# A two-layer fp32 decoder trunk: new opening and last unit, sums by adding DMAs, two more seven-product pairs and new orders

## The chip, the cores and the metric

The kernel runs on one core of a Trainium2 chip. Times are microseconds on the device, of whole executions; the profile shows one execution. In the text TensorE is PE in the rows, VectorE is DVE, ScalarE is ACT, GpSimd is POOL and SyncE is SP. GpSimd issues the DMAs that convert a type or add into their destination; the other DMAs are issued by SyncE, or ScalarE.

## The reference, cut to what matters

Two layers over 256 rows x of 2048 values, all in float32. Almost all of the work is in the matrix products: w_in (2048 x 6160), w_o (2048 x 2048), w_up (2048 x 8192) and w_down (8192 x 2048) in each layer. Every value is asked for to float32 accuracy.

```python
def hybrid_layer(x, ...):
    h = rms_norm(x, attn_norm)
    proj = jnp.einsum('bsd,de->bse', h, w_in)
    g_q, g_k, g_v, g_gate, g_lr, s_q, s_k, s_v = jnp.split(proj, COL_SPLITS, axis=-1)
    ...
    mixed = jnp.concatenate([o_gla, o_sb], axis=-1)
    x = x + jnp.einsum('bse,ed->bsd', mixed, w_o)
    hm = rms_norm(x, mlp_norm)
    up = jnp.square(jax.nn.relu(jnp.einsum('bsd,df->bsf', hm, w_up)))
    return x + jnp.einsum('bsf,fd->bsd', up, w_down)
```

## The kernel before

**A float32 product is three matmuls.** Operand and weight are each split in a rounded high part and the low part that the rounding left. High by high, high by low weight and low by high weight are summed in a PSUM bank (lines 630 to 632 in the opening, 1231, 1234 and 1235 in the planned part), each a 128x512 matmul. High parts (whi) are made by ScalarE, low parts (wlo) by VectorE with one subtraction. The weights of two pairs in each unit are split by DMA instead: a casting DMA makes chi (line 1059), ScalarE copies it negated into dlo (line 1063), and a DMA that adds the weight to dlo leaves the low part there (line 1066). GpSimd issues both in program order.

**Units, pairs and steps.** A unit is 2048 rows of a weight by 1024 columns: eight pairs of 128-row blocks, into up to eight PSUM banks. A pair takes eight products (24 matmuls, two steps) or, as a "fast" pair, seven (21 matmuls, four steps): products of sums of blocks, in the way of Strassen and Winograd, for which VectorE makes one sum of 128x1024 and two of 128x512 (line 876) and some more low parts. The operand's sums are made once for each of its pairs and kept (table `FAST_OF` by operand: `ht` for h, `sxh` and `sx` for the MLP's). The banks of a fast unit aren't yet results: the unit's tail adds them into four quarters of 128x512, two row halves by two column halves.

**The tables set the order.** A table for each kind of unit (`EACH`, `FEWER`, `LATER`, `O0`, `O1`, `OWN`) holds the order of the steps by pair number, the fast pairs, and the pairs that are split by DMA. `LATER` is for the key and query units `ik` and `iq` that run at the end of layer 0 and belong to layer 1's input product (around 1110 to 1190 us). The class `Plan` (line 63) takes the pieces of all units with their lengths and due times. PE, SP and POOL follow the order in which the program names their pieces; VectorE and ScalarE take, of the pieces that can start, the one that is due first.

**The drain of a down unit.** `seeded_tail` (line 1295) first puts x's own values into banks 2, 4, 3 and 8 (seeds). When the products are done, ScalarE copies bank 1 into x11, VectorE makes the difference dw of bank 6 and x11 in a temporary (one of `T2` = 5), and so on in `sums`; `half` (one for each column half c) adds banks 2 and 3 on VectorE, and copies banks 4 and 8 on ScalarE, after which VectorE adds bank 5 to the latter and dw to both. In the last unit of the kernel each quarter is stored from there (line 1346).

**The opening.** x, the gains (line 337) and the first weights are loaded on SP's queue in this order. `wait_on_x(WARM0)` lets TensorE turn the identity 8 times. `norm_operand` (line 507 for the turns, 517 for the high parts on ScalarE, 523 for the low ones on VectorE) makes the first two blocks of h out of x; between its turns and its high parts `turn_gains` (line 346) turns the gains into columns. `wait_on_x(WARM1)` is 13 more turns of the identity (line 580). Then come the first products.

Of the kernel before, what the change touches and what calls it, by code (L numbers as in the profile page):

```python
# [11 lines left out]
F32R = mybir.dt.float32r  # L12
BF16 = mybir.dt.bfloat16
AF = mybir.ActivationFunctionType
ALU = mybir.AluOpType
# [1 line left out]

P = 128
EPS = 1e-6
WARM0, WARM1 = 8, 13  # L20
T2 = 5
FAST = (1, 3, 5, 6)
EACH = [7, 7, 1, 1, 0, 1, 2, 5, 2, 5, 5, 3, 5, 3, 3, 4, 6, 1, 6, 6, 6, 3, 4, 0], FAST, (2, 4)
FEWER = [0, 0, 2, 1, 1, 1, 4, 1, 7, 7, 6, 6, 2, 6, 6, 3, 3, 3, 5, 3, 4, 5], (1, 3, 6), (2, 4)
LATER = [4, 0, 0, 1, 1, 4, 1, 1, 3, 3, 3, 2, 6, 3, 6, 6, 6, 5, 5, 5, 5, 2, 7, 7], FAST, (2, 4)
FAST_OF = {"ht": FAST, "sxh": (0, 1, 3, 5, 6), "sx": (0, 1, 3, 5, 6)}
TWO_WAYS = (("sxh", 0), ("sx", 0))
O0 = [4, 4, 7, 7, 6, 6, 0, 0, 0, 0, 5, 1, 1, 1, 2, 5, 1, 2, 2, 2, 3, 3], (0, 1, 2), (5, 7)
O1 = [4, 5, 4, 2, 2, 2, 2, 6, 1, 1, 0, 0, 1, 1, 0, 0, 6, 5, 7, 7, 3, 3], (0, 1, 2), (5, 6)
SEEDED = (("down", 0), ("down", 1), ("o", 1))  # L30
SPARE = ("sxh",)
OWN = {
    ("up", 0): ([2, 6, 6, 6, 6, 3, 3, 3, 3, 4, 1, 1, 5, 1, 2, 1, 5, 5, 5, 0, 4, 0, 0, 0, 7, 7], (0, 1, 3, 5, 6), (2, 4)),
    ("up", 0, 0): ([0, 0, 1, 4, 1, 1, 5, 1, 5, 2, 3, 5, 3, 3, 5, 2, 3, 6, 6, 6, 6, 4, 7, 7], FAST, (2, 4)),
    ("up", 1): ([0, 0, 3, 3, 4, 3, 3, 5, 5, 5, 6, 5, 2, 6, 6, 6, 1, 1, 2, 1, 1, 7, 4, 7], FAST, (2, 4)),
    ("down", 0): ([0, 0, 3, 3, 1, 4, 3, 3, 1, 5, 1, 2, 1, 5, 5, 5, 2, 6, 6, 6, 6, 4, 7, 7], FAST, (2, 4)),
    ("down", 1): ([7, 7, 3, 3, 2, 3, 3, 1, 1, 1, 2, 1, 0, 0, 0, 0, 5, 5, 4, 5, 5, 6, 6, 6, 6, 4], (0, 1, 3, 5, 6), (2, 4)),
}
CAST, AHEAD_BY = 3, 1
FIRST_RAWS = 6  # L40
RING, LOWS, ADDS, RAWS = 5, 4, 2, 3
# [21 lines left out]
class Plan:  # L63
# [29 lines left out]
    def run(self):  # L93
# [20 lines left out]
        line = {e: [p for p in self.pieces if p.engine == e] for e in ("PE", "SP", "POOL")}  # L114
# [3 lines left out]
        ready = {"DVE": [], "ACT": []}  # L118
        order, events, count = [], [], 0
        left_tiles, sure = T2, 0  # L120
        for p in self.pieces:
# [53 lines left out]
def trunk_kernel(  # L175
# [90 lines left out]
    def f32(ap):  # L266
        return ap.bitcast(F32)

    nc.scalar.preload_act_table_set("natural_log_exp_and_others")


    ident = cpool.tile([P, P], F32, name="ident")
# [178 lines left out]
    def forms(op, i, t, tag):  # L451

        both = (tag, i) in TWO_WAYS
        keep = tag is None or both

        e = []
        todo = []

        a11, a21, a12, a22 = (t[:, k, r * P : (r + 1) * P] for k in range(2) for r in range(2))

        def new(k):
            if not e:
                n = 4 if keep else 3
                e.append(tmp("t2", [P, 512], bufs=T2)[:, : n * P].rearrange("p (k c) -> p k c", c=P))
            return a21 if k == 3 and not keep else e[0][:, k, :]

        def sums(k):
            a, b = ((a21, a11), (a21, a22), (a11, new(3)), (a12, new(0)))[k]  # L470
            nc.vector.tensor_tensor(new((2, 3, 0, 1)[k]), a, b, ALU.subtract)

        def high():
            if e:
                if both:
                    if tag in SPARE:
                        op.x[i] = act_tile(F32R, (P, 4, 2, P))
                    else:
                        op.x[i] = tmp(tag + "k", [P, 4, 2, P], F32R, bufs=1)
                elif keep:  # L480
                    op.x[i] = act_tile(F32R, (P, 4, 2, P))
                else:
                    op.x[i] = tmp(tag, [P, 3, 2, P], F32R, bufs=4)
# [375 lines left out]
    def ordered(l, units, hT, rst, ug, gates_t, mixed=None, ons=None):  # L859
# [23 lines left out]
        def unit_order(u):  # L883

            kind, q, n2 = units[u]
            if kind == "g":
                return [i // 2 for i in range(8)], (), ()
            if kind == "o":
                return (O0, O1)[n2]
            if u and units[u - 1][0] == "down" and kind == "iv":  # L890
                return FEWER
            if l >= 0 and kind in AHEAD:
                return LATER
            return OWN.get((kind, n2, q), OWN.get((kind, n2), EACH))

        def added(u, j):
# [398 lines left out]
        def seeded_tail(u):  # L1295
            kind, q, n2 = units[u]
            end = kind == "down" and q == 3 and l + 1 == DEPTH
            x11, x21, x12, x22 = (
                (lambda ap=xb[2 * n2 + c][:, tt, :]: ap) for c in range(2) for tt in range(2)
            )  # L1300
# [13 lines left out]
            def sums(p):  # L1314
# [6 lines left out]
                b = vector(dw, bk(7), dw, a, p[7])  # L1321
                free.update({1: [c], 6: [w], 5: [a], 7: [b]})
                box["s"] = (w, b, a, b)

            def half(c, p):
                got = []
                for tt, (m, dst) in enumerate((((2, x11), (4, x21)), ((3, x12), (8, x22)))[c]):
                    before = [p[m], seeds[m]]
# [324 lines left out]
    his = []  # L1653
    load_x(0, parts=2)
    load_gains(0, (("attn", attn_norm, KT),))
    wait_on_x(WARM0)
    st["first"] = norm_operand(hT, 0, "attn", 0, lambda: turn_gains(0))
    wait_on_x(WARM1)
# [316 lines left out]
```

## Time and profile before

| | us |
|---|---|
| median of 3 runs | 2124.44 |
| lowest and highest of them | 2122.53, 2124.86 |
| time of the profiled execution | 2122.05 |
| its span in the trace | 2120.2 |
| TensorE busy in it | 2111.3 |

The span counts from the first to the last event of the trace. The profiled execution's own time is 1.85 us more than its span, which lies around it. TensorE's time counts a 128x512 matmul with 0.39 us, though the next begins earlier: rates are to be read from one start to the next.

### The profile page before, as it was taken

To read this page: it belongs to the slowest core of one execution; us is meant where nothing else is said; L and a number is where in the kernel's file an instruction comes from. 1 tells how busy PE (TensorE), PEld (TensorE's weight loads), DVE (VectorE), ACT (ScalarE), POOL (GpSimd) and SP (SyncE) were. 2 spreads that over 40 slices of the span, in tenths; PEclk is the share of its full clock that TensorE was granted. 3 is DMA by queue.
4 is the path that set the end of the run, shared out by engine and by line. 5 is a ranking of instruction groups with operands and counts; after the bars stand their busy time and mean duration, and the time that the engine had idled before them with its cause. 6 is when DMAs were issued, how large, how long until landed. Compare 5 with 4: busy or idle time off the path is not lost.

```text
span 2120.2 us, 28343 instructions
## 1 busy us (share of the span) xinstructions
PE 2111.3 (100%) x10040; PEld 1758.5 (83%) x10040; DVE 1936.9 (91%) x2658; ACT 1498.6 (71%) x2032; POOL 273.6 (13%) x394
## 2 busy tenths in 40 slices
PE   9999999999999999999999999999999999999998
PEld 7888888888888888888888888888888888888887
DVE  6988769999999999999998886799999999999998
ACT  7667667777677677677776665677776776776775
POOL 1110001111111111111111000111112111111110
PEclk9999999999999999999999999999999999999999
DMA  9865367888888988988998644778889888889886
GB/s 318 257 184 188 111 198 221 231 268 260 250 245 246 263 250 251 258 258 244 253 266 240 189 138 135 211 220 252 259 244 255 261 251 254 245 250 261 249 253 191
DMA packets 157618, 497.15 MB, mean 234 GB/s; under 512 B 10682, under 2 KB 19458, under 8 KB 157476
## 3 DMA queue, kind: packets, MB, share of 16 engines
q1 hardware_dynamic: 100900, 319.16, 42.2%
q0 software_dynamic: 56576, 176.18, 37.0%
q8 instruction: 79, 1.29, 0.2%
q14 instruction: 63, 0.52, 0.1%
HBM read 493.20 MB, written 2.10 MB: 234 GB/s over the span
## 4 chain that ended last, share of the span: by engine, by line
PE 76%; issue 17%; POOL 2%; DVE 1%; DMA 1%; ACT 1%; POOLq 0%; ACTq 0%
PE acc L630 3%; PE acc L632 3%; PE acc L631 3%; POOL dlo L1066 1%; POOL chi L1059 1%; DMA raw<-in_w_up_dram 1%; DMA dlo<-in_w_down_dram 1%; DVE wlo L613 0%; PE ps L741 0%; PE ps L759 0%; PE ps L1912 0%; ACT whi L611 0%; DVE t L1767 0%; PE ps L1862 0%; PE ps L795 0%
## 5 line engine op out<-in xcount | busy, mean ns | idle before, releaser
L1102 DVE TENSOR_TENSOR wlo<-raw,whi 128x1024 fp32r<-128x1024 f32 (+1 forms) x697 | 751.2, 1084 | 67.9 <-ACT whi L1098 45.5
L1098 ACT ACTIVATE whi<-raw 128x1024 fp32r<-128x1024 f32 (+1 forms) x697 | 648.3, 946 | 193.3 <-DVE raw L876 83.0
L1063 ACT ACTIVATE dlo<-chi 128x1024 fp32r<-128x1024 f32 x168 | 177.7, 1058 | 106.5 <-DMA chi<-in_w_down_dram 12.7
L1098 ACT ACTIVATE whi<-ts 128x1024 fp32r<-128x1024 f32 x177 | 187.6, 1060 | 84.2 <-DVE ts L876 69.9
L1102 DVE TENSOR_TENSOR wlo<-ts,whi 128x1024 fp32r<-128x1024 f32 x177 | 215.7, 1219 | 4.7 <-PE m__244_1205 L1234 2.7
L876 DVE TENSOR_TENSOR ts<-raw 128x1024 f32<-128x1024 f32 x177 | 215.8, 1219 | 2.7 <-DMA raw<-in_w_up_dram 1.8
L630 PE MATMUL acc<-whi,act 128*128 128x512 f32 (+2 forms) x384 | 141.3, 368 | 0.0
L632 PE MATMUL acc<-whi,act 128*128 128x512 f32 (+2 forms) x384 | 136.7, 356 | 0.0
L631 PE MATMUL acc<-wlo,act 128*128 128x512 f32 (+2 forms) x384 | 136.4, 355 | 0.0
L611 ACT ACTIVATE whi<-raw 128x1024 fp32r<-128x1024 f32 (+2 forms) x98 | 88.5, 909 | 64.4 <-PE acc L632 63.4
L613 DVE TENSOR_TENSOR wlo<-raw,whi 128x1024 fp32r<-128x1024 f32 (+2 forms) x98 | 100.4, 1031 | 30.0 <-ACT whi L611 29.2
L876 DVE TENSOR_TENSOR raw<-raw 128x512 f32<-128x512 f32 x177 | 121.5, 686 | 1.5
L876 DVE TENSOR_TENSOR raw<-ts,raw 128x512 f32<-128x512 f32 x177 | 121.2, 685 | 0.3
L1059 POOL DMA_DIRECT2D chi<-in_w_up_dram x64 | 38.1, 595 | 507.5 <-PE m__2882_13580 L1235 29.6
L1059 POOL DMA_DIRECT2D chi<-in_w_down_dram x64 | 38.5, 601 | 453.1 <-PE m__3280_15441 L1235 21.9
L630 PEld LDWEIGHTS acc<-whi,act 128*128 128x128 f32 x384 | 72.5, 189 | 12.2 <-issue 3.4
L632 PEld LDWEIGHTS acc<-whi,act 128*128 128x128 f32 x384 | 72.3, 188 | 10.4
L631 PEld LDWEIGHTS acc<-wlo,act 128*128 128x128 f32 x384 | 72.5, 189 | 9.0 <-DVE wlo L613 0.2
L1419 ACT ACTIVATE act<-act,st 128x512 f32<-128x512 f32 x88 | 61.9, 718 | 24.6 <-DVE act L876 24.2
L1066 POOL DMA_DIRECT2D dlo<-in_w_down_dram x64 | 59.6, 931 | 127.8 <-ACT dlo L1063 121.6
L1066 POOL DMA_DIRECT2D dlo<-in_w_up_dram x64 | 58.2, 909 | 65.4 <-ACT dlo L1063 57.5
L492 DVE TENSOR_TENSOR act<-t,act 128x512 fp32r<-128x512 f32 x94 | 63.9, 685 | 0.0
(4536 smaller groups left out, 5800.2 us busy)
## 6 DMA issues: line engine op xcount, KB each, us to landing
raw<-in_w_up_dram SPq DMA_DIRECT2D x96, 1024.0 KB, 6.8
raw<-in_w_down_dram SPq DMA_DIRECT2D x96, 1024.0 KB, 7.8
raw<-in_w_in_dram SPq DMA_DIRECT2D x72, 1024.0 KB, 6.6
chi<-in_w_up_dram POOLq DMA_DIRECT2D x64, 512.0 KB, 5.2
dlo<-in_w_up_dram POOLq DMA_DIRECT2D x64, 512.0 KB, 7.9
chi<-in_w_down_dram POOLq DMA_DIRECT2D x64, 512.0 KB, 7.2
dlo<-in_w_down_dram POOLq DMA_DIRECT2D x64, 512.0 KB, 9.2
raw<-in_w_o_dram SPq DMA_DIRECT2D x24, 1024.0 KB, 7.9
```

Source lines behind the costliest of these rows:

```text
L492: nc.vector.tensor_tensor(d[:, :, 1, :], src, f32(d[:, :, 0, :]), ALU.subtract)
L611: newest["hi"] = nc.scalar.activation(h, r, AF.Copy).ins
L613: newest["lo"] = nc.vector.tensor_tensor(lo[:, q : q + step, :width], r, f32(h), ALU.subtract).ins
L630: nc.tensor.matmul(o, xh[:, sl], whi[:, j, :width], start=first, stop=False)
L631: nc.tensor.matmul(o, xh[:, sl], wlo[:, j, :width], start=False, stop=False)
L632: st["mm"] = nc.tensor.matmul(o, xl[:, sl], whi[:, j, :width], start=False, stop=last).ins
L876: nc.vector.tensor_tensor(dst, a, b, op)
L1059: nc.gpsimd.dma_start(flat("h"), src)
L1063: nc.scalar.activation(box["l"], f32(box["h"]), AF.Copy, scale=-1.0)
L1066: nc.gpsimd.dma_start(flat("l"), src, accum_op=ALU.add)
L1098: nc.scalar.activation(box["h"][:, :n], src(), AF.Copy)
L1102: nc.vector.tensor_tensor(box["l"][:, :n], src(), f32(box["h"][:, :n]), ALU.subtract)
```

## The change

It has four parts. *Opening:* the gains go on ScalarE's DMA queue, and its table of functions is loaded behind that; their turn stands ahead of the turns of x; `WARM1` is 4 in place of 13. *Last unit:* it has its own order, `LAST`, and a tail `last_half` in which x22 is made up in advance (bank 5 and dw added to x), so that bank 8 is added last, in two halves of 256 columns, each stored by its own DMA; the copies on ScalarE are left out there. *Sums by DMA:* in the other twelve down units with q < 3, `late_half` lets ScalarE copy banks 2 and 3 to temporaries, and three adding DMAs on POOL's queue (line 1362) add those two and dw into x in place of three additions on VectorE. POOL's pieces are then taken by due time. *Tables:* `LATER` and `FAST_OF["ht"]` have a fifth fast pair, and nearly all orders are new.

```diff
-WARM0, WARM1 = 8, 13
+WARM0, WARM1 = 8, 4
-LATER = [4, 0, 0, 1, 1, 4, 1, 1, 3, 3, ...], FAST, (2, 4)
-FAST_OF = {"ht": FAST, ...}
+LATER = [2, 0, 0, 0, 3, 2, 0, 3, 4, 3, ...], (0, 1, 3, 5, 6), (2, 4)
+FAST_OF = {"ht": (0, 1, 3, 5, 6), ...}
+LAST = [7, 7, 6, 6, 6, 6, 2, 1, 1, 1, 4, 1, 5, 5, 5, 0, 0, 2, 0, 3, 3, 3, 5, 0, 3, 4], (0, 1, 3, 5, 6), (2, 4)
...
-            nc.sync.dma_start(
+            (nc.sync if b else nc.scalar).dma_start(
                 graw[b][r : r + DEPTH * n, :], src.rearrange("l (k p) -> (l k) p", p=P)
             )
...
         if between:
+            got = between()
             for part in both:
                 part[0]()
-            got = between()
...
+            def last_half(c, p):
...
+                            combine(
+                                dst()[:, cols], banks[m][:, cols], a[:, cols],
+                                ALU.subtract if m == 4 else ALU.add,
+                            )
+                            c0 = n * 512
+                            nc.sync.dma_start(
+                                ov[:, tt, c0 + cols.start : c0 + cols.stop], xb[n][:, tt, cols]
+                            )
...
+            def late_half(c, p):
+                got = []
+                for tt, (m, dst) in enumerate((((2, x11), (4, x21)), ((3, x12), (8, x22)))[c]):
+                    def copy(m=m, dst=dst, tt=tt):
+                        if not tt:
+                            box[m] = tmp("t2", [P, 512], bufs=T2)
+                        nc.scalar.activation(dst() if tt else box[m], banks[m], AF.Copy)
+
+                    def more(m=m, dst=dst):
+                        src = dw() if m == 8 else box[m]
+                        nc.gpsimd.dma_start(dst(), src, accum_op=ALU.add)
+
+                    a = add("ACT", A1, copy, p[m], seeds[m], take=1 - tt)
+                    free[m] = [a]
+                    if m == 8:
+                        a = vector(x22, bk(5), x22, a, p[5])
+                        free[5] = free[5] + [a]
+                    if m == 4:
+                        got.append(vector(x21, x21, dw, a, box["s"][1], op=ALU.subtract))
+                        box["4"] = got[-1]
+                        continue
+                    got.append(add("POOL", 1.0, more, a, box["s"][2 * c + tt], lag=ADD))
```

The first place is TensorE's opening. The rows are matmuls, in the order of its program; those of `ident` alone are warm-up turns, those of `ident,xb` turn x, that of `ident,t` turns the gains. Before:

```order
L580 MATMUL ps_100<-ident 128x128 x8
L507 MATMUL ps_109<-ident,xb_91 128x128 x4
L507 MATMUL ps_114<-ident,xb_91 128x128 x4
L346 MATMUL ps_119<-ident,t_4_98 128x32
L580 MATMUL ps_131<-ident 128x128 x13
L630 MATMUL acc_145<-whi_151,act_122 128x512
L631 MATMUL acc_145<-wlo_152,act_122 128x512
```

And of the change (the lines are one further down in its code):

```order
L581 MATMUL ps_100<-ident 128x128 x8
L347 MATMUL ps_109<-ident,t_4_97 128x32
L508 MATMUL ps_112<-ident,xb_90 128x128 x4
L508 MATMUL ps_117<-ident,xb_90 128x128 x4
L581 MATMUL ps_131<-ident 128x128 x4
L631 MATMUL acc_136<-whi_142,act_122 128x512
L632 MATMUL acc_136<-wlo_143,act_122 128x512
```

The turn of the gains moved ahead of the turns of x, and nine warm-up turns between them and the first product are gone.

The second place is POOL's queue in layer 0 where the down unit of the second column half ends and the next up unit begins. chi and dlo are weights of the up unit, split by DMA; rows of xb are sums of the down unit's drain. Before:

```order
L1059 DMA chi_5353<-in_w_up_dram 128x1024
L1066 DMA dlo_5355<-in_w_up_dram 128x2x512
L1059 DMA chi_5439<-in_w_up_dram 128x2x512
L1066 DMA dlo_5441<-in_w_up_dram 128x1024
L1059 DMA chi_5457<-in_w_up_dram 128x1024
L1066 DMA dlo_5501<-in_w_up_dram 128x2x512
```

And of the change:

```order
L1062 DMA chi_5334<-in_w_up_dram 128x2x512
L1069 DMA dlo_5336<-in_w_up_dram 128x2x512
L1362 DMA xb_92<-t_1136_5366 128x512
L1362 DMA xb_93<-t_1148_5424 128x512
L1062 DMA chi_5436<-in_w_up_dram 128x1024
L1069 DMA dlo_5440<-in_w_up_dram 128x2x512
L1062 DMA chi_5462<-in_w_up_dram 128x1024
L1362 DMA xb_93<-t_1146_5414 128x512
L1069 DMA dlo_5511<-in_w_up_dram 128x1024
```

Two sums stand between dlo_5336 and the casting DMA behind which the next low part (dlo_5440) is made, and one more stands ahead of dlo_5511.

The third place is VectorE's end, in the last unit. m__ names are PSUM banks, t is the temporary dw, and xb_93 and xb_94 are the two quarters' column blocks (xb_92 and xb_93 in the change). Before:

```order
L876 TENSOR_TENSOR t_4128_19416<-m__4095_19228,xb_93 128x512
L876 TENSOR_TENSOR xb_94<-m__4084_19184,t_4128_19416 128x512
L876 TENSOR_TENSOR xb_93<-m__4069_19103,xb_93 128x512
L876 TENSOR_TENSOR t_4128_19416<-m__4087_19192,t_4128_19416 128x512
L876 TENSOR_TENSOR xb_94<-m__4072_19126,xb_94 128x512
L876 TENSOR_TENSOR xb_93<-xb_93,t_4128_19416 128x512
L876 TENSOR_TENSOR xb_94<-m__4084_19184,xb_94 128x512
L876 TENSOR_TENSOR xb_94<-xb_94,t_4128_19416 128x512
```

And of the change:

```order
L877 TENSOR_TENSOR t_4165_19476<-m__4129_19273,xb_92 128x512
L877 TENSOR_TENSOR xb_93<-m__4121_19250,t_4165_19476 128x512
L877 TENSOR_TENSOR xb_92<-m__4107_19171,xb_92 128x512
L877 TENSOR_TENSOR t_4165_19476<-m__4124_19259,t_4165_19476 128x512
L877 TENSOR_TENSOR xb_93<-m__4121_19250,t_4165_19476 128x512
L877 TENSOR_TENSOR xb_93<-m__4111_19202,xb_93 128x512
L877 TENSOR_TENSOR xb_92<-m__4108_19180,t_4165_19476 128x512
L877 TENSOR_TENSOR xb_93<-m__4114_19217,xb_93 128x256 x2
```

Before, the last two operations add bank 5 (m__4084) and dw to the quarter into which ScalarE has copied bank 8. Now bank 5 (m__4121) goes into that quarter three rows ahead of the end, and the last row is bank 8 (m__4114) added in two halves of 256 columns.

## Rows read from the trace of the kernel before

**Rows 1.** The head of the page: span, and busy time with share and instructions.
```profile
span 2120.2 us, 28343 instructions
...
PE 2111.3 (100%) x10040; PEld 1758.5 (83%) x10040; DVE 1936.9 (91%) x2658; ACT 1498.6 (71%) x2032; POOL 273.6 (13%) x394
```

**Rows 2.** TensorE's waits, 10 to 2115 us: operation, releaser: sum, times, longest.
```profile
PE ps L741 <- DVE act L704: 1.1, 2, 0.5
PE m__1856_8735 L1438 <- DVE act L876: 0.2, 1, 0.2
```

**Rows 3.** Timeline, opening: start, duration, engine, line, operation [idle before <- releaser].
```profile
1.83 0.46 SPq L337 DMA_DIRECT2D t<-in_attn_norm_dram  x1
...
2.33 1.84 SPq L600 DMA_DIRECT2D raw<-in_w_in_dram  x4
...
3.88 1.97 PE L507 MATMUL ps<-ident,xb 128*128 128x128 f32 x8 [0.47 <-DMA xb<-in_x_dram]
...
6.02 3.03 PE L580 MATMUL ps<-ident 128*128 128x128 f32 x13
...
6.36 1.57 ACT L517 ACTIVATE act<-ps,gcol_a 128x256 fp32r<-128x256 f32 x4 [4.25 <-DVE gcol_a L347]
...
7.80 2.28 ACT L611 ACTIVATE whi<-raw 128x512 fp32r<-128x512 f32 x4
...
8.71 0.78 PE L630 MATMUL acc<-whi,act 128*128 128x512 f32 x1
...
9.08 0.87 DVE L523 SCALAR_TENSOR_TENSOR act<-ps,gcol_a,act 128x256 fp32r<-128x256 f32 x2
...
9.61 0.39 PE L632 MATMUL acc<-whi,act 128*128 128x512 f32 x1
...
9.84 0.39 PE L630 MATMUL acc<-whi,act 128*128 128x512 f32 x1
...
11.92 1.03 PE L507 MATMUL ps<-ident,xb 128*128 128x128 f32 x8
```

**Rows 4.** Timeline of the end, from 2114 us.
```profile
2114.40 0.39 PE L1235 MATMUL m__4077_19151<-chi,act 128*128 128x512 f32 x1
...
2114.82 0.60 ACT L1332 ACTIVATE xb<-m__4077_19151 128x512 f32<-128x512 f32 x1 [2.12 <-PE m__4077_19151 L1235]
...
2116.18 0.69 DVE L876 TENSOR_TENSOR xb<-xb,t 128x512 f32<-128x512 f32 x1
```

**Rows 5.** The stores of x (one line's instructions): duration ns min/median/max, starts.
```profile
L1346 SPq DMA_DIRECT2D out_dram<-xb x8: 332/332/367, 2072.0 to 2116.9; - x8
...
DMA to landing us min/median/max: 2.1/2.1/2.1
```

**Rows 6.** Low weight parts made by adding DMAs, whole span; who waited.
```profile
L1066 POOL DMA_DIRECT2D dlo<-in_w_down_dram x64: 833/846/1222, 473.1 to 2095.6; - x64
...
  PEld m__1302_6143 L1234: 0.5, 1
```

**Rows 7.** The same tiles around 565 us: an issue, its use, issue to landing.
```profile
566.80 0.88 POOL L1066 DMA_DIRECT2D dlo<-in_w_up_dram  x1 [0.84 <-ACT dlo L1063]
...
L1234 PE MATMUL m__1145_5429<-dlo,act x3: 389/389/389, 565.0 to 577.2; 128*128 128x512 f32 x3
...
DMA to landing us min/median/max: 6.1/6.5/9.0
```

**Rows 8.** GpSimd's DMA queue on the page: packets, MB, share of 16 engines.
```profile
q0 software_dynamic: 56576, 176.18, 37.0%
```

**Rows 9.** Two windows: busy PE, PEld, DVE, ACT, POOL; clock; DMA share; GB/s.
```profile
600.00:640.00 40.00, 40.00 (x187) 33.28 (x186) 39.72 (x56) 30.05 (x39) 4.20 (x6) 1.00 0.78 237
...
1110.00:1150.00 40.00, 40.00 (x179) 33.11 (x178) 36.43 (x40) 26.46 (x30) 6.72 (x8) 1.00 0.94 251
```

**Rows 10.** The page's groups of VectorE: sums and low parts of seven-product pairs.
```profile
L876 DVE TENSOR_TENSOR ts<-raw 128x1024 f32<-128x1024 f32 x177 | 215.8, 1219 | 2.7 <-DMA raw<-in_w_up_dram 1.8
...
L876 DVE TENSOR_TENSOR raw<-raw 128x512 f32<-128x512 f32 x177 | 121.5, 686 | 1.5
```

More of the change, by code (lines that the diff above doesn't have):

```diff
@@ L32 @@
 OWN = {
[L33 to L37, printed above, removed]
-}
+    ("up", 0): ([2, 6, 6, 6, 6, 5, 5, 5, 5, 2, 3, 3, 3, 1, 3, 4, 1, 1, 4, 1, 0, 0, 0, 0, 7, 7], (0, 1, 3, 5, 6), (2, 4)),
+    ("up", 0, 0): ([0, 0, 3, 3, 1, 3, 2, 3, 2, 1, 1, 1, 6, 6, 6, 6, 4, 5, 5, 5, 5, 7, 7, 4], FAST, (2, 4)),
+    ("up", 1): ([0, 0, 3, 3, 3, 2, 3, 1, 1, 1, 6, 1, 4, 6, 6, 6, 5, 5, 2, 5, 5, 7, 7, 4], FAST, (2, 4)),
+    ("down", 0): ([0, 0, 1, 1, 4, 1, 3, 1, 2, 3, 3, 6, 3, 6, 6, 4, 6, 5, 5, 5, 5, 2, 7, 7], FAST, (2, 4)),
+    ("down", 1): ([7, 7, 3, 3, 3, 3, 2, 1, 1, 1, 4, 1, 6, 6, 6, 6, 0, 2, 0, 0, 5, 5, 0, 5, 5, 4], (0, 1, 3, 5, 6), (2, 4)),
+}
+LAST = [7, 7, 6, 6, 6, 6, 2, 1, 1, 1, 4, 1, 5, 5, 5, 0, 0, 2, 0, 3, 3, 3, 5, 0, 3, 4], (0, 1, 3, 5, 6), (2, 4)
+LATE_SUMS = True
 CAST, AHEAD_BY = 3, 1
@@ L113, in run @@
                 p.due = min([u.due for u in p.users], default=t) - p.length - p.lag - self.GAP
-        line = {e: [p for p in self.pieces if p.engine == e] for e in ("PE", "SP", "POOL")}
+        line = {e: [p for p in self.pieces if p.engine == e] for e in ("PE", "SP")}
         free = dict.fromkeys(("PE", "SP", "POOL", "DVE", "ACT"), 0.0)
@@ L117, in run @@
         at = dict.fromkeys(self.pieces, 0.0)
-        ready = {"DVE": [], "ACT": []}
+        ready = {"DVE": [], "ACT": [], "POOL": []}
         order, events, count = [], [], 0
@@ L267, in f32 @@
         return ap.bitcast(F32)
-    nc.scalar.preload_act_table_set("natural_log_exp_and_others")
     ident = cpool.tile([P, P], F32, name="ident")
@@ L482, in high @@
                 else:
-                    op.x[i] = tmp(tag, [P, 3, 2, P], F32R, bufs=4)
+                    op.x[i] = tmp(tag, [P, 3, 2, P], F32R, bufs=len(set(FAST_OF[tag]) - {j for a, j in TWO_WAYS if a == tag}))
                 todo.append((op.x[i], e[0]))
@@ L893, in unit_order @@
                 return LATER
+            if l + 1 == DEPTH and u + 1 == len(units):
+                return LAST
             return OWN.get((kind, n2, q), OWN.get((kind, n2), EACH))
@@ L1297, in seeded_tail @@
             end = kind == "down" and q == 3 and l + 1 == DEPTH
+            last = l + 1 == DEPTH and u + 1 == len(units)
+            late_sums = LATE_SUMS and kind == "down" and q < 3
             x11, x21, x12, x22 = (
@@ L1323, in sums, with fn @@
                 box["s"] = (w, b, a, b)
+                if last:
+                    box["s"] = (w, b, a, vector(x22, bk(5), dw, b, p[5], seeds[8]))
+            def last_half(c, p):
+                for tt, (m, dst) in enumerate((((2, x11), (4, x21)), ((3, x12), (8, x22)))[c]):
+                    n, parts = 2 * n2 + c, 2 if m == 8 else 1
+                    for i in range(parts):
+                        def fn(m=m, dst=dst, tt=tt, cols=slice(i * 512 // parts, (i + 1) * 512 // parts)):
+                            a = dw() if m == 4 else dst()
+                            combine(
[6 more added lines that the diff above has]
+                            )
+                        add(
+                            "DVE", V1 / parts, fn, p[m], seeds[m], box["s"][2 * c + tt],
+                            box["s"][3] if m == 4 else [], give=m == 4,
+                        )
@@ new lines, in late_half @@
+            def late_half(c, p):
+                got = []
+                for tt, (m, dst) in enumerate((((2, x11), (4, x21)), ((3, x12), (8, x22)))[c]):
+                    def copy(m=m, dst=dst, tt=tt):
[15 more added lines that the diff above has]
+                    got.append(add("POOL", 1.0, more, a, box["s"][2 * c + tt], lag=ADD))
+                    add("POOL", 0.0, None, got[-1], box["4"] if m == 8 else [], give=1)
+                x_done[2 * n2 + c] = got
@@ L1325, in half @@
             def half(c, p):
+                if last:
+                    return last_half(c, p)
+                if late_sums:
+                    return late_half(c, p)
                 got = []
@@ L1655, in trunk_kernel @@
     load_gains(0, (("attn", attn_norm, KT),))
+    nc.scalar.preload_act_table_set("natural_log_exp_and_others")
     wait_on_x(WARM0)
```

10 lines of the change are left out of this document (5 added, 5 removed).

## Prediction

> **What bounds the kernel now.** I begin with the head of the page: TensorE is busy 2111.3 of 2120.2 us, VectorE 91% and ScalarE 71% of the span [rows 1]. Before looking for waits I ask whether TensorE has any. Its waits between 10 and 2115 us, that is all of the kernel but its two ends, are three and sum to 1.3 us [rows 2]. Weights that are made by an adding DMA, the latest operands here, made it wait three times more, 0.5 us at most [rows 6]. So in the middle nothing but the number of products sets the time: 0.227 us from one 128x512 product to the next, which is the step from 9.61 to 9.84 between two products in the opening's timeline [rows 3]. All other work is cover, and an edit there is worth nothing unless it removes products or makes one wait. What is left are the ends: 8.71 us before the first product, and 2120.2 - 2114.40 = 5.8 us from the start of the last product to the end of the span.
>
> In the opening the reader is to follow the row of the first product back: product 8.71 <- rounding of the weights on ScalarE from 7.80 <- four roundings of h from 6.36 <- the gain's columns, which VectorE copies behind the turn of the gains; ScalarE had idled 4.25 us for them [rows 3]. The gains were issued at 1.83, behind x, and the weights at 2.33. In the tail: product 2114.40 <- nothing; behind it a ScalarE copy (2114.82), two operations of VectorE until 2116.18 + 0.69 = 2116.87, and the last store at 2116.9, 2.1 us until it lands [rows 4, 5].
>
> **The change, part by part.**
>
> *Products.* One more seven-product pair in the key and in the query unit of layer 0's end takes 3 matmuls from each: -6 x 0.227 = -1.36 us, on the path. For it VectorE makes one 128x1024 sum (1.22), two 128x512 sums (0.69 each) and about 1.5 us more of low parts [rows 10]: 4.1 us in each unit of some 40 us. The window of the first of them shows VectorE busy 36.4 of 40 us [rows 9], so 40.5 after. That is more than full by the count. But the window from 600 to 640 us, where other units run, shows 39.7 of 40 with TensorE busy all 40.00 [rows 9], so this load alone doesn't stall products. I take nothing for it; the upper bound is the excess over 40, 0.5 in each of the two, 1 us.
>
> *Tail.* The new last unit makes the last quarter of x in advance but for one bank, and adds that bank from PSUM in two halves of 256 columns, each with its own store. Instead of a copy and two full operations (2114.82 to 2116.87) there are two additions of half size. A 128x256 operation on VectorE takes 0.87 for two in the opening [rows 3], half of 0.69 would be 0.35 each [rows 4]. So the end of the arithmetic comes at 2114.82 + 0.70...0.87 = 2115.5 to 2115.7 in place of 2116.87: -1.2 to -1.35. The last store is half as large; what it saves of 2.1 us no row says, from nothing to 0.2 I guess. The store waits for SP, whose issue takes 0.33 [rows 5], and a store of the first half may be in its way: up to +0.3. I take -1.2 (-0.9 to -1.5). It needs the VectorE chain of the other banks to be done by then: 21 matmuls follow the last product into banks 1 and 6 now, where it was 15, so the seven operations ahead of the halves (7 x 0.69 = 4.8 us at most) have 21 x 0.227 = 4.8 us; the +0.3 of the range covers that too.
>
> *Opening.* The gains are issued by ScalarE's queue at about 0.8 instead of behind x at 1.83, and the turn of the gains stands ahead of the x transposes. The raw weights move forward on SP by the gains' 0.46 to 0.50 (1.83 to 2.33) [rows 3]. The 4.25 us idle time of ScalarE then ends with the transposes: the x transposes, eight in 1.97, from 3.88 or some 0.3 later for the turn of the gains; the four roundings of 1.57 are ready from about 5.3 in place of 6.36, and done by 7.0 in place of 7.80. Then the weights must be there. No row shows when they land; in the profile ScalarE went over to them at 7.80 without idling, so they landed before. If they are what comes last, the gain is at least the 0.5 of the issue; if not, 7.80 - 6.6 = 1.2 at most. I take -0.6 (0 to -1.2).
>
> Against it stand nine warm-up transposes fewer. The eight x transposes of the opening take 1.97, the eight at 11.92 take 1.03 [rows 3]: the array ran at the lower of its two levels (1.2 GHz) at first and at the upper (2.4) later, and the products were at 0.227 from 9.61 on. In between the array did nothing but 13 warm-up transposes (6.02 to 9.05) with the first product in their wake. With four, its transposes end about 7.1 (x from 4.2 for 1.97, then four at 0.23), and it stands idle up to the first product at 8.1. If the upper level comes later for that, each product up to there costs 0.227 more. The bounds: nothing, and all twelve products ahead of the transposes of 11.92, 12 x 0.227 = 2.7 us. I take the middle, +1.3, since the rows hold no other rise to compare. The opening is then +0.7 (-1.2 to +2.7).
>
> *Adding DMAs into x, and the orders.* In twelve down units three sums of the drain leave VectorE: -2.1 us of its time per unit, which is no time on the path. ScalarE has two copies more, at 71%. The price is on the queue of adding and casting DMAs, which GpSimd issues in program order: each sum waits there for ScalarE's copy and VectorE's last sum into the same part of x, and behind it stand the next unit's casting and adding weight transfers, for which TensorE waits in the end. A weight transfer that stands behind two of them starts later by two issues of 0.85 [rows 6] and by two transfers. The queue took 37.0% of the span for 176.18 MB [rows 8], 784 us, so 4.45 us per MB, 1.17 us for the 256 KB of one sum: 2 x (0.85 + 1.17) = 4.0 us. At this place before, the transfer issued at 566.80 lands 6.5 later (the median there) at 573.3 and is used at 577.2: 3.9 us of slack [rows 7]. The two cancel to 0.1. The order after gives such transfers somewhat more room between the last use of their buffer and their own use, so I count them as hidden. From below: the 1.3 and 0.5 us of present waits could go, together at most -2; from above, six such transitions late by 1 us or more. I take +0.3 (-2 to +6).
>
> **A rule beside this row.** The trace shows 64 issues of the down weights' adding DMAs with 833 / 846 / 1222 ns (least, median, most) [rows 6], while VectorE was busy nine tenths of the time: the median is 13 ns above the least. The Trainium skill (page "DMA: Bandwidth & Descriptors", section "SWDGE vs HWDGE vs iDMA") has descriptors of such DMAs written by GpSimd into SBUF, where VectorE locks it out in its two-port mode. By it an added issue could wait a whole VectorE instruction, 1.22 us at most, and the two issues would cost 2.4 in place of 1.7 us: 0.7 late at each of the six places, 4 us in all. The row speaks for the rare exception, and the sum keeps 0.85.
>
> **Sum.** -1.36 - 1.2 + 0.7 + 0.3 = -1.6 against the profiled execution's own 2122.05: 2120.5. The three runs shown have a median of 2124.44, 2.4 above it; where a run of the new kernel will fall in that spread is open, so I add half: 2121.7.
>
> **Rivals.** What a measurement of this kernel tells from no change is about 0.2%, 4.2 us.
> *A, the sum above* (chance 0.50): 2120 to 2123.5.
> *B, the clock doesn't suffer* (0.20): the transposes before and between keep the array at its level, the opening gives its 0.6, so -2.9: 2120.4 with the same half. For it speaks that the rise before came with only transposes behind it; against it the idle stretch of about 1 us that is new.
> *C, slower: sums ahead of tight weights* (0.10): in the down-to-up transitions the two adding DMAs stand ahead of a weight transfer. It decides from 3.9 us: beyond it each us is one of TensorE's, six times. If the issues wait for VectorE or the transfers for a busy ring (the share in 1110 to 1150 is 0.94 [rows 9]; landing there takes up to 9.0 [rows 7]), 1 to 2 us late at six places, less 1.6: +4.4 to +10, 2126 to 2132. Against it: the new order has some more room there.
> *D, relief* (0.12): VectorE at 91% is what makes runs vary, and 12 x 2.1 us less of it, and reordered units, take the waits away that the slower runs have: to the bottom of both spreads, 2117 to 2119.5.
> *E, the opening eats the rest* (0.08): all twelve products at the lower level, +2.7 - 0.6, and with the tail and the products nothing is left: 2122 to 2124.5. This is also how it looks where the change does nothing measurable at all.
>
> **Numbers.** The time is A's, 2121.7. From D's upper part to the lower edge of C: 2117.5 to 2127, which leaves out half of C, a part of D and little else; A alone is 2120 to 2123.5. Faster than 2124.44 by over 4.2 us means below 2120.2: most of D (0.10), half of B (0.10) and a tenth of A (0.05), 0.25. Slower, above 2128.7: 0.08, nearly all from C. The rest, 0.67, is within.
>
> **What would show it.** Products: fewer matmul rows by six, and no new TensorE waits between 1110 and 1190; VectorE there near 40 of 40. Tail: last matmul to the end of the span 4.6 in place of 5.8, and two 128x256 additions behind it. Opening: ScalarE's 4.25 us of idle gone, first product near 8.1, and its first twelve products spaced 0.45 (clock late) or 0.227. Sums: the weights made by adding DMAs still have under 1 us of TensorE waits in all, and TensorE's waits between 10 and 2115 stay near 1.3. What would make it wrong: a list of waits for adding DMAs at the six transitions of 1 us or more each, or a VectorE that is late in the key and query units, where its load comes to the full 40 us. Either would show as a TensorE wait with VectorE or a DMA as the releaser, of a length that is missing in the trace before.

## The result, and the profile after

The changed kernel takes 2128.66 us (median of 22 runs, 2124.04 to 2134.33) against 2123.51 for the kernel before on the same chips: a ratio of 1.0024, 95% interval [1.0018, 1.0030]. It is slower by 5.1 us where 2121.7 and no measurable change were forecast. (Of all executions timed here one, of e9 below, took 2873.65 us; it is left out of the ratio.) The profiled execution took 2128.84, with a span of 2126.0: 5.8 us more than [rows 1]. The head of its page:

```profile
span 2126.0 us, 28470 instructions
...
PE 2110.8 (99%) x10025; PEld 1754.3 (83%) x10025; DVE 1928.7 (91%) x2637; ACT 1513.8 (71%) x2060; POOL 322.9 (15%) x430
```

TensorE's rows are 15 fewer, the six matmuls and the nine turns. Its busy time falls by half a microsecond only, and the span is longer: it now waits. The list of its waits from 10 to 2120 us (operation, releaser: sum, times, longest) answers to [rows 2]:

```profile
PE m__3224_15100 L1237 <- DMA dlo<-in_w_up_dram: 1.6, 1, 1.6
PE ps L742 <- DVE act L705: 1.1, 2, 0.5
PE m__623_2919 L1237 <- DMA dlo<-in_w_o_dram: 1.0, 1, 1.0
PE m__1158_5464 L1237 <- DMA dlo<-in_w_up_dram: 0.8, 1, 0.8
PE m__1469_6906 L1237 <- DMA dlo<-in_w_up_dram: 0.6, 1, 0.6
PE m__157_788 L1237 <- DVE wlo L1105: 0.4, 1, 0.4
PE m__2900_13592 L508 <- DVE xb L877: 0.4, 1, 0.4
PE m__3864_18056 L1237 <- DMA dlo<-in_w_up_dram: 0.3, 1, 0.3
PE m__83_428 L1237 <- DVE wlo L1105: 0.2, 1, 0.2
PE m__1789_8384 L1237 <- DMA dlo<-in_w_up_dram: 0.2, 1, 0.2
PE m__3553_16614 L1237 <- DMA dlo<-in_w_up_dram: 0.2, 1, 0.2
```

1.3 us have become 6.8, and 4.7 of these are waits for dlo, the low parts of weights that an adding DMA makes. Of the seven, six belong to up units that follow a down unit of the second column half, the places of rival C; the other is an output unit (m__623). Around the fourth in the list, m__1158 at 580 us, the timeline of GpSimd and SyncE has these rows (start, duration, operation [idle before <- releaser]):

```profile
556.46 1.20 POOL L1069 DMA_DIRECT2D dlo<-in_w_up_dram  x1
...
557.40 0.37 SPq L1026 DMA_DIRECT2D raw<-in_w_up_dram  x1
...
560.87 0.37 SPq L1026 DMA_DIRECT2D raw<-in_w_up_dram  x1
...
564.74 0.88 POOL L1362 DMA_DIRECT2D xb<-t  x1 [7.08 <-DVE t L877]
...
566.75 0.86 POOL L1362 DMA_DIRECT2D xb<-t  x1 [1.12 <-issue]
```

The lines at 564.74 and 566.75 are two sums into x. The dlo ahead of them and the dlo behind them (issued at 568.10) land as follows (the tile's issue, then issue to landing):

```profile
L1069 POOL DMA_DIRECT2D dlo<-in_w_up_dram x1: 1202/1202/1202, 556.5 to 556.5; - x1
...
DMA to landing us min/median/max: 10.0/10.0/10.0
...
L1069 POOL DMA_DIRECT2D dlo<-in_w_up_dram x1: 1279/1279/1279, 568.1 to 568.1; - x1
...
DMA to landing us min/median/max: 11.7/11.7/11.7
```

Before, the second one took 6.5 us [rows 7], and the first one this:

```profile
L1066 POOL DMA_DIRECT2D dlo<-in_w_up_dram x1: 1193/1193/1193, 557.4 to 557.4; - x1
...
DMA to landing us min/median/max: 6.1/6.1/6.1
```

After the change the first lands at 566.5 and the second at 579.8, and TensorE starts with each within 0.1 us: it was waiting, 0.8 us for the second and under 0.2 for the first, which the list leaves out. The first has no sum ahead of it, but two weight loads of 1 MB that SyncE issues 0.9 and 4.4 us behind it; before, one was issued 5.0 us ahead of it and one 2.2 behind. By this the list divides: four of the waits (m__3224, m__1469, m__3864, m__1789; 2.7 us) are for an up unit's first dlo, two (m__1158, m__3553; 1.0 us) for its second, the one behind two sums, and one (1.0 us) is in the output unit, where no sum is near.

The list understates the loss. From the x turns behind the opening to the last product (11.14 to 2120.50 in the rows below, 11.92 to 2114.40 in [rows 3, 4]) the changed kernel takes 6.9 us longer with 1.4 us of products less, so 8.3 are lost there, where the list has 5.5 more than before. At m__1158, for one, TensorE's steps from start to start are 1.1 us too long for a listed wait of 0.8.

The timeline of the two ends, for [rows 3] and [rows 4, 5]:

```profile
5.48 1.69 ACT L518 ACTIVATE act<-ps,gcol_a 128x256 fp32r<-128x256 f32 x4 [2.89 <-PE ps L508]
...
7.06 1.15 ACT L612 ACTIVATE whi<-raw 128x512 fp32r<-128x512 f32 x2
...
7.74 0.50 PE L631 MATMUL acc<-whi,act 128*128 128x512 f32 x1 [0.59 <-ACT whi L612]
...
11.14 1.03 PE L508 MATMUL ps<-ident,xb 128*128 128x128 f32 x8
...
2120.50 0.39 PE L1238 MATMUL m__4114_19217<-chi,act 128*128 128x512 f32 x1
...
2120.93 0.76 DVE L877 TENSOR_TENSOR xb<-m__4114_19217,xb 128x256 f32<-128x256 f32 x2
```

The first product starts at 7.74 (8.71 before) and the x turns at 11.14 (11.92). ScalarE's idle time ahead of the roundings of h is 2.89 us (4.25), and from them it goes over to the weights at 7.06 without idling. From the last product to the end of the span it is 5.5 us (5.8).

### The profile page after: what moved, and what is told of

Read it like the earlier page. It is cut to its first block, busy times and chain, and to the rows that moved or that the text cites. A ratio compares the mean times of both kernels' runs of the same rounds, so it can differ in the third digit from the quotient of the medians.

```text
span 2126.0 us, 28470 instructions
## 1 busy us (share of the span) xinstructions
PE 2110.8 (99%) x10025; PEld 1754.3 (83%) x10025; DVE 1928.7 (91%) x2637; ACT 1513.8 (71%) x2060; POOL 322.9 (15%) x430
## 4 chain that ended last, share of the span: by engine, by line
PE 86%; DMA 5%; issue 4%; DVE 3%; ACT 2%; POOL 1%; DVEq 0%; POOLq 0%; ACTq 0%
DMA dlo<-in_w_up_dram 3%; PE acc L631 2%; PE acc L633 2%; PE acc L632 2%; DMA raw<-in_w_in_dram 1%; DVE wlo L1105 1%; DMA dlo<-in_w_o_dram 1%; ACT whi L612 1%; DVE wlo L614 0%; PE ps L742 0%; ACT act L518 0%; POOL chi L1062 0%; PE ps L760 0%; PE ps L1969 0%; DVE t L1824 0%
## 5 line engine op out<-in xcount | busy, mean ns | idle before, releaser
L1105 DVE TENSOR_TENSOR wlo<-ts,whi 128x1024 fp32r<-128x1024 f32 x179 | 218.1, 1218 | 11.4 <-PE m__626_2922 L1237 1.2
L1062 POOL DMA_DIRECT2D chi<-in_w_up_dram x64 | 43.4, 678 | 397.4 <-PE m__824_3911 L1234 21.5
L1069 POOL DMA_DIRECT2D dlo<-in_w_up_dram x64 | 66.3, 1037 | 97.3 <-ACT dlo L1066 92.0
```

The costliest lines, as they stand in the source:

```text
L1062: nc.gpsimd.dma_start(flat("h"), src)
L1069: nc.gpsimd.dma_start(flat("l"), src, accum_op=ALU.add)
L1105: nc.vector.tensor_tensor(box["l"][:, :n], src(), f32(box["h"][:, :n]), ALU.subtract)
```

## The experiments

Each run was timed against the kernel before on its own chip. In brackets is the 95% interval of the ratio. 0.001 is 2.1 us. In the expectations the "queue theory" is that the adding DMAs into x make the weights behind them late; its rival, the "orders theory" or "second theory", is that the new orders do it. The "six transitions" are the places where a down unit of the second column half is followed by an up unit. Each run has one profile, of one execution.

**One part at a time.** The opening, the last unit, the pairs and the sums, each alone in the kernel before, with its old orders:

```diff
 e1   WARM1 = 13 -> 4, gains on ScalarE's queue, their turn first
 e2   LAST and last_half
 e3   LATER and FAST_OF["ht"]
 e4   late_half, POOL by due time
```

> The kernel before with the new opening alone (gains on ScalarE's queue, their turn first, 4 warm-up turns). Queue theory (the adding DMAs into x make the weights behind them late; all else gains or is neutral): -0.8 us, ratio 0.9996, first product at 7.7, turns of the next x block at 11.1, products spaced 0.23 from the third on, so no price for the fewer warm-up turns. The prediction's own term, +0.7 with products at half rate, would give the x turns at 12.6. Orders theory says the same as the queue theory here.

> The kernel before with the new order and tail of the last unit alone. If the stores crowd each other (three quarters stored within 2.5 us of the end): from the start of the last product to the end of the span 5.5 in place of 5.8, ratio 0.9999. If the prediction's term holds: 4.6, ratio 0.9994. Queue and orders theories say nothing else of it.

> The kernel before with five seven-product pairs in the key and query units and their new order alone. Six matmuls fewer: -1.4 us, ratio 0.9993, if VectorE and the weight DMAs keep up; TensorE's waits between 1110 and 1190 as before, under 0.5 us. If VectorE is full there: waits of 1 to 2 us on wlo, ratio 1.0000 or above. Queue and orders theories: 0.9993.

> The kernel before, with its old orders, and three sums of each of twelve down units by adding DMAs (queue taken by due time). Queue theory: TensorE waits for dlo behind the second column half's down units, 0.3 to 1.8 us at each of six places, 4 to 7 us in all, ratio 1.002 to 1.003. Orders theory (the sums are hidden; the new orders make the weights late): ratio 0.9995 to 1.0005 and waits as before.

Measured: e1 1.0006 [0.9997, 1.0015], e2 0.9999 [0.9990, 1.0008], e3 1.0006 [0.9997, 1.0015], e4 1.0036 [1.0022, 1.0049]. The sums alone cost more than the whole change. TensorE's waits for dlo in e4:

```profile
PE m__1470_6917 L1236 <- DMA dlo<-in_w_up_dram: 1.4, 1, 1.4
PE m__3212_15084 L1236 <- DMA dlo<-in_w_up_dram: 0.9, 1, 0.9
PE m__1790_8395 L1236 <- DMA dlo<-in_w_up_dram: 0.8, 1, 0.8
PE m__1150_5439 L1236 <- DMA dlo<-in_w_up_dram: 0.8, 1, 0.8
```

All four are the second dlo of an up unit behind a down unit, the one with two sums ahead of it. The queue theory stands for the old orders. In e2 the end is as forecast, 4.66 us from the last product (2115.64) to the end of the span (2120.3). In e1 the first product is as early as in the changed kernel (7.80), but then (two products; and a window: busy PE with its count of instructions, PEld, DVE, ACT, POOL, clock, DMA share, GB/s):

```profile
10.41 0.63 PE L633 MATMUL acc<-whi,act 128*128 128x512 f32 x1
10.83 0.63 PE L631 MATMUL acc<-whi,act 128*128 128x512 f32 x1
...
10.00:12.00 2.00, 2.00 (x6) 1.62 (x5) 1.06 (x2) 0.59 (x2) 0.00 (x0) 1.00 1.05 402
```

From 9.13 to 12.08 a product starts each 0.43 us, where it took 0.227 before. That is the spacing that e6, below, has at the lower granted clock; the clock column of this early window says 1.00 and doesn't resolve it. The x turns come at 12.77, later than the 11.92 before, though the first product was 0.9 earlier. Both bounds of the prediction occur: the changed kernel's own profile had almost none of this, e1 most of it, and e10, below, all (13.31). e3 was not faster; its profile has two dlo that came 2.0 and 2.1 us late (at 1016 us, in a down unit, and at 1124, in the key unit), but whether its other executions had them isn't known.

**Undoing the sums, and halving them**, in the changed kernel with all its new orders:

```diff
 e5  -LATE_SUMS = True
     +LATE_SUMS = False
 e6   late_sums = ... q < 3 and n2 == 0
 e7   late_sums = ... q < 3 and n2 == 1
 e8  -nc.gpsimd.dma_start(dst(), src, accum_op=ALU.add)
     +nc.gpsimd.dma_start(dst()[:, :32], src[:, :32], accum_op=ALU.add)
```

> The changed kernel with LATE_SUMS off: all sums of the drains stay on VectorE, new orders, opening, last unit and pairs stay. Queue theory (the adding DMAs into x make the weights behind them late): the waits for dlo at the six transitions are gone, 5 to 7 us below the changed kernel, ratio to the kernel before 0.9990 to 1.0000. Orders theory (the new orders make the weights late): still 1.0015 or more, with waits for dlo at the same six places.

> The changed kernel with adding DMAs only for the six down units of the first column half (18 of the 36); the other units' sums on VectorE. If the place behind the second half's units is the cost: as without any, 0.9990 to 1.0000, no waits for dlo at the six transitions. If the volume of added transfers is the cost: half of the loss stays, about 1.0010 to 1.0015.

> The changed kernel with adding DMAs only for the six down units of the second column half, ahead of the next up unit's weights. If the place is the cost: all of the loss, 1.002 to 1.003, waits of 0.3 to 1.8 us at the six places. If the volume is: half of it, about 1.0010 to 1.0015.

> The changed kernel with each of the 36 adding DMAs cut to 32 of 512 columns (the rest of these sums is left out): as many issues and the same order, a sixteenth of the bytes. If the price is the transfers' time in the queue and on the DMA engines: the waits go, 0.9990 to 1.0000. If it is the issues on GpSimd and the order (two issues of 0.86 and the wait of the first for VectorE): the waits stay, 1.0015 to 1.003.

Measured: e5 1.0015 [1.0006, 1.0023], e6 1.0032 [1.0020, 1.0045], e7 1.0018 [1.0009, 1.0027], e8 1.0014 [1.0005, 1.0023]. Without any sum by DMA the kernel is still slower than before: the queue theory alone falls. And the place doesn't decide as I thought: the sums of the first column half cost no less than those of the second, with waits of 2.4 and 2.2 us at the first dlo of two up units. Why there is not settled; at both places SyncE issued its loads closer behind the dlo (0.3 us behind it, and level with it, in place of 0.9), and the dlo landed 12.0 and 11.4 us after its issue. With thin sums (e8) the time is that without: what they cost on top of the new orders goes with the bytes, but this is 0.0009 or 0.0010 between intervals that overlap.

e6 shows what a longer wait brings. Windows ahead of and behind the wait that ended at 735.4 (columns as above):

```profile
731.00:734.00 3.00, 1.93 (x8) 1.04 (x6) 2.94 (x5) 1.53 (x2) 0.58 (x1) 1.00 1.04 346
...
735.00:739.00 4.00, 3.58 (x9) 2.86 (x10) 2.43 (x3) 1.06 (x1) 0.46 (x1) 0.57 1.03 240
```

The granted clock falls to 0.57 behind the wait, and in the 4 us TensorE starts 9 matmuls where 17 fit at 0.227. A wait of 2.4 us costs 4.2 in all (from the starts of its matmuls: 2.7 in the step itself, and 1.5 in seven further steps that are longer by 0.17 to 0.37 each).

**The orders.** e9 is the kernel before with all new orders but that of the key and query units. e10 is the changed kernel without the sums and with the old orders of up, down and output units; e11 is e10 with the old opening, and e12 is e10 with 13 warm-up turns. In e9 to e12 POOL's pieces are in program order again, in e5 still by due time; by the names of the tiles the order of the weights' DMAs is the same.

> The kernel before with the new orders of all units but the key and query ones, and nothing else (no adding DMAs into x, old opening, last unit and pairs). Second theory, in which the orders cost by themselves because three 1 MB weight loads go out together just behind the first adding DMA of an up unit: ratio 1.0010 to 1.0020, waits for dlo of 0.2 to 1.5 us at the six places where a down unit is followed by an up unit, and that DMA lands 10 us behind its issue in place of 6. Queue theory alone: 0.9990 to 1.0005 and landings as before.

> The changed kernel without adding DMAs into x and with the old orders of the up, down and output units; new opening (4 warm-up turns), last unit, five pairs and the new order of the value unit stay. If orders and sums are all of the loss: 0.9990 to 1.0000. If the opening costs too (upper clock level at 12 in place of 9 us): 0.9995 to 1.0005, x turns near 12.6.

> As the run before, with the old opening. If the new opening costs more than it gains: 0.5 us faster than with it, 0.9988 to 0.9995 of the kernel before. If it gains 0.8 us: 0.8 us slower than with it.

> As the run before the last, new opening but with 13 warm-up turns as before. If it is the idle array that delays the upper clock level: x turns at 11.2 to 12.0, the level reached at 9 or earlier, and the first product at 7.8 to 9.1 (13 turns take 1.4 to 3.0). If the delay has nothing to do with the turns: the level at 11.5 to 12 as with four, and x turns near 13.5.

Measured: e9 1.0015 [1.0006, 1.0024], e10 0.9988 [0.9979, 0.9997], e11 0.9990 [0.9981, 0.9999], e12 0.9989 [0.9980, 0.9998]. The orders alone cost 3.2 us. e5, which adds to them the parts that gain in e10, is no faster than e9; the intervals leave room for that gain. The first dlo of the up unit, SyncE's loads around it, and issue to landing, in e9 and then in e10:

```profile
557.74 1.19 POOL L1068 DMA_DIRECT2D dlo<-in_w_up_dram  x1
...
558.87 0.37 SPq L1025 DMA_DIRECT2D raw<-in_w_up_dram  x1
...
562.35 0.37 SPq L1025 DMA_DIRECT2D raw<-in_w_up_dram  x1
...
DMA to landing us min/median/max: 9.8/9.8/9.8
```

```profile
554.58 0.37 SPq L1026 DMA_DIRECT2D raw<-in_w_up_dram  x1
...
559.27 1.19 POOL L1069 DMA_DIRECT2D dlo<-in_w_up_dram  x1 [1.13 <-issue]
...
562.54 0.37 SPq L1026 DMA_DIRECT2D raw<-in_w_up_dram  x1
...
DMA to landing us min/median/max: 6.4/6.4/6.4
```

In e9 two loads are issued behind the dlo while it is under way, 1.1 and 4.6 us behind its issue, much as in the changed kernel, and the dlo takes 9.8 us. (The expectation has three that go out together; the third is issued at 571.84, when the dlo has landed.) In e10, with the old orders, one went out 4.7 us ahead of the dlo and one 3.3 behind it, and the dlo takes 6.4. All eighteen profiles divide like this at the six transitions: in the six with the new orders of up and down units (the changed kernel, e5 to e9) both loads are behind the first dlo, and it lands 9.2 to 12.0 us after its issue; in the eleven with the old order of one or both, one load is behind it, and it takes 6.1 to 8.8; e13 has both behind it and takes 8.0 to 11.1. All waits of e10 between 10 and 2110 us:

```profile
PE ps L742 <- DVE act L705: 1.1, 2, 0.5
```

e10 is the version that beats both kernels, by 2.5 us the one before; its parts are the opening, the last unit, the pairs and the value unit's new order, and without the opening (e11) it is 2.1. Its end is as forecast, 4.65 us from the last product (2114.45) to the end of its span (2119.1):

```profile
2114.45 0.39 PE L1238 MATMUL m__4090_19169<-chi,act 128*128 128x512 f32 x1
```

e12's array didn't idle ahead of its first product; its x turns came at 11.18, e10's at 13.31. Yet the two take the same time, and so does e11.

**Which orders, and bytes or issues** (e13: the kernel before with the new orders of the up units of the first half and the down units of the second; e14: those up units alone; e15: e10 with the sums; e16: e15 with sums cut as in e8):

> The kernel before with the new orders of two kinds of unit alone: the up units of the first column half and the down units of the second, which meet at the six transitions. If the loss of the new orders sits at these places: ratio 1.0010 to 1.0015, dlo landing 10 us behind its issue at 557 us and waits there. If it is in the output and value units: 0.9995 to 1.0005 and landings near 6.

> The kernel before with the new order of the up units of the first column half alone. If the weight loads that go out together are brought about by what the down unit ends with: 0.9995 to 1.0005, landings near 6 at 557 us. If they are by what the up unit begins with: 1.0010 to 1.0015 and landings near 10.

> The changed kernel with the old orders of the up, down and output units, and with the adding DMAs into x. Beside the same kernel without them (0.9988): if the sums cost more with the old orders, as the run of the sums alone says, 1.0015 to 1.0025. If they cost as with the new ones, 0.9 thousandths: 0.9995 to 1.0000.

> As the run before, each adding DMA cut to 32 of 512 columns (the rest of these sums is left out). If the bytes are the price here too: 0.9985 to 0.9993. If the issues and their order are: 1.0005 to 1.0025.

Measured: e13 1.0059 [1.0046, 1.0071], e14 1.0017 [1.0008, 1.0025], e15 1.0032 [1.0021, 1.0044], e16 0.9997 [0.9988, 1.0006]. e13 loses four times what all orders together lose, by waits for dlo and for VectorE's sums into x: an order is no part that has a price of its own. e14 loses as much as all orders though its first dlo land after 6.4 to 8.0 us; its listed waits are elsewhere (the longest 1.0, for a dlo of a down unit). So the new up order alone doesn't bring both loads behind the dlo (with the down order, in e13, it does), and not every loss of an order is made by them. Beside e10 the sums cost 0.0044 with their bytes and 0.0009 without. The dlo behind two sums, in e15 and then in e16:

```profile
L1069 POOL DMA_DIRECT2D dlo<-in_w_up_dram x1: 952/952/952, 567.9 to 567.9; - x1
...
DMA to landing us min/median/max: 11.6/11.6/11.6
```

```profile
L1069 POOL DMA_DIRECT2D dlo<-in_w_up_dram x1: 959/959/959, 570.0 to 570.0; - x1
...
DMA to landing us min/median/max: 8.7/8.7/8.7
```

11.6 us from issue to landing with full sums, 8.7 with thin ones; in e10 it is 6.1. The bytes make about half of the delay (2.9 of 5.5 here; the means of the six transitions are 11.2, 9.0 and 6.2), and most of the time lost; 0.0009 is again between intervals that overlap.

**The six transitions, summed.** The starts of TensorE's matmuls in the traces say where the time goes: what the steps from one 128x512 matmul to the next take beyond 0.227 us, summed over the six transitions, around the use of the first dlo (5 to 15 us behind its issue) and of the second (15 to 30 us behind the same issue), in us:

| | first dlo | second dlo |
|---|---|---|
| before; e10 (old orders, no sums) | 0.1; 0.2 | -0.1; -0.1 |
| e4; e15 (old orders, sums) | -0.1; -0.1 | 5.3; 6.5 |
| e16 (old orders, thin sums) | -0.1 | -0.1 |
| e9; e5 (new orders, no sums) | 5.0; 4.7 | -0.1; -0.1 |
| e8 (new orders, thin sums) | 5.3 | -0.1 |
| the changed kernel; e7 (new orders, sums ahead of up units) | 4.3; 4.3 | 2.1; 2.6 |

The two causes stand apart: the new orders cost at the first dlo, with or without sums, and the sums at the second, with full bytes only. Of the 8.3 that the changed kernel loses, 4.2 more than before are at the first and 2.2 more at the second; 1.3 are in the output unit, at 313 us (e9 loses 1.2 there too, e10 with its old order nothing). The table is of one execution for each kernel. e6 (8.9 and 0.1) loses all of it at the first, and e14 (1.2 and 0.6) most of its loss elsewhere.

## Why the prediction was wrong, step by step

**The step that failed** is the last of the sum, "adding DMAs into x, and the orders", +0.3. It holds two errors.

*The orders were taken as free*, since they leave more room from a dlo's issue to its use. They do: the first dlo of the up unit had 7.6 us before (issued at 557.4, in the row above; first used at 565.0, the first of the uses in [rows 7]) and has 9.9 in the changed kernel. But its landing takes 10.0 in place of 6.1. The prediction took the slack of the second dlo, 3.9, for the place, and never that of the first, which the trace before gives as 565.0 - 557.4 - 6.1 = 1.5. e9 measures the orders: 1.0015, 3.2 us, and its profile loses 5.0 at the first dlo. That SyncE's loads delay it is read from where they stand in the eighteen profiles; no run varied them alone.

*The sums were priced 4.0 us a place, against 3.9 of slack*, and called hidden; the tie was the sign to give rival C more than one chance in ten. What they did shows beside e5, which has the same orders and no sums. Its second dlo is issued at the same 568.1 (issue, first use, landing):

```profile
L1069 POOL DMA_DIRECT2D dlo<-in_w_up_dram x1: 1172/1172/1172, 568.1 to 568.1; - x1
...
L1237 PE MATMUL m__1152_5452<-dlo,act x2: 389/389/389, 579.1 to 579.8; 128*128 128x512 f32 x2
...
DMA to landing us min/median/max: 6.8/6.8/6.8
```

It lands at 574.9, 4.2 us ahead of its use. With the sums it lands at 579.8, 4.9 later, and TensorE waits 0.8. So slack and price were near, and the sum came out on the wrong side of the tie. Their make-up was not as priced: the two issues of 0.85 added nothing, as the dlo is issued at the same time; with thin sums (e8) the dlo of this place lands after 9.3 us, so 2.4 of the 4.9 go with the bytes, as 2 x 1.17 said; the other 2.5 stay with thin sums, and no run shows what makes them. (SyncE's load is one candidate: with sums, thin or full, one is issued 1.3 us ahead of this dlo, in e5 it is 2.5 behind.) In time the price of the sums rests on the orders: 0.0044 with the old ones (e15 beside e10) and 0.0009 with the new ones (the changed kernel beside e5, where the intervals overlap). Rival C named the mechanism, the places and a range, 2126 to 2132, that holds the result; it missed that the orders alone lose two thirds as much.

The rest of the sum stood: without this term it is -1.9 against the kernel before, and e10, which leaves out the sums and most of the new orders, measures -2.5 (its interval is -4.5 to -0.6).

**Products, -1.36:** right by the rows, six fewer; no time shows it alone (e3). In the changed kernel's profile TensorE waited for nothing between 1110 and 1190 us, and VectorE is at 37.5 and 39.1 of 40, where the prediction counted 40.5. Its windows:

```profile
1110.00:1150.00 40.00, 40.00 (x178) 33.02 (x177) 37.50 (x44) 25.66 (x30) 6.70 (x8) 1.00 0.96 257
1150.00:1190.00 40.00, 40.00 (x178) 33.12 (x177) 39.06 (x47) 25.76 (x32) 6.28 (x15) 1.00 0.65 185
```

**Tail, -1.2:** right in the trace: 4.66 us behind the last product in e2, where it is alone, and 4.65 in e10, against 5.8. In the changed kernel it is 5.5. There the record of the last stretch has one instruction load of 0.01 MB behind the stores, as in e8 (5.6); the other nine profiles with the new last unit, at 4.65 to 4.74, have none. Whether that load is the cause wasn't tried.

**Opening, +0.7 (-1.2 to +2.7):** right in kind. In nine profiles with four turns the x turns came at 11.1 to 13.4 us, 12.6 in the mean; in eight with the old opening at 11.6 to 12.6, 12.05 in the mean. So the new opening takes 0.5 more than it gives, with a wide spread. The fewer turns are the likely cause: in seven of the nine at least five of the first twelve products start 0.43 us behind the one ahead, in the nine profiles with 13 turns (e12 is one of them) none does. The time doesn't show it: e10, e11 and e12 agree within their intervals. The bound of -1.2 for the gain rests on 7.80 - 6.6, and no row gives the 6.6; with the 7.0 of its own text it would be 0.8. The first product came 0.97 earlier.

**The rule on GpSimd's descriptors** (the Trainium skill, "DMA: Bandwidth & Descriptors", section "SWDGE vs HWDGE vs iDMA") isn't borne out by the sums' issues: the 36 of the changed kernel took 828 / 864 / 1108 ns (least, median, most) beside a VectorE at nine tenths, much as the row had it. The dlo issues of 1.2 us above are no witness for it either: they are those of 128x2x512, which took 1.19 us before too (the line of 557.4 above), and the 0.88 of [rows 7] is one of 128x1024.

## What to carry to other kernels

Where TensorE never waits, every transfer on a tight list has a slack. List the slack of each one at the place, not of one alone (here 1.5 and 3.9 us), and price a new transfer or a new order by what it puts beside the others too: the landing itself moves (6.1 to 10.0 us here), not only the room. A part that gains nothing but relief on an engine that is not the bound (VectorE here) can only lose when it pays with the resource that has no slack. When tables of orders are tuned together, test the parts apart, and the orders apart from them: here the opening, the last unit and the pairs together were 2.5 us faster (e10), and with the sums and the new orders the kernel was 5.1 slower. The prices of the parts don't simply add up (e13, and the sums with the old and the new orders).

## What the runs showed of the hardware that was not expected

Two adding DMAs of 256 KB within SBUF, with what moved beside them, made the weight transfer behind them land 11.6 us after its issue where 6.1 was the time without (e15, e10). Cut to a sixteenth of the bytes, the two still made it 8.7 (e16). So 2.9 go with the bytes here, and 2.2 in the mean of the six transitions: 1.5 and 1.1 for each, near the queue's mean time for as many, 1.17. The rest of the delay, 2.6 here, doesn't.

An adding DMA of 512 KB landed 6.1 to 8.8 us after its issue where one load of 1 MB was issued on SyncE's queue while it was under way, and 9.2 to 12.0 where two were, one within 1.1 us and one within 4.6 (the changed kernel and e5 to e9; in e13, also with two, 8.0 to 11.1).

Waits of TensorE of 2.1 (e3), 2.4 (e6) and 2.7 us (e15) had a lower granted clock behind them (0.57, 0.61 and 0.65 in the 4 us behind each), others of 2.0 (e3) and 2.2 us (e6) did not (1.00 behind them). Nor did products 0.43 us apart follow any wait of the changed kernel, the longest of which is 1.6.
